# A two-layer GELU network on one core: the second matmul of the first superblocks as one pipeline with a pinned vector order, and a new start

## The chip, the cores and the metric

The kernel runs on one core of a Trainium2 chip. The metric is the device time of one execution in microseconds (us). The kernel before takes 1579.98 us (median of 3 runs, 1578.31 to 1580.16). The profile is of one execution; its span is about 2 us shorter than that execution's time. Engines: PE is the matmul engine, DVE the vector engine, ACT the scalar engine, POOL the general-purpose engine, SP the engine whose queue issues most loads.

## The reference

```python
# x: 8 x 1024 x 1024, w1: 1024 x 4096, w2: 4096 x 1024, all float32
h = x @ w1
h = 0.5 * h * (1 + np.tanh(np.sqrt(2 / np.pi) * (h + 0.044715 * h ** 3)))
return (h @ w2).astype(np.float32)
```

## The kernel before

The 8192 rows of x are handled in eight superblocks of 1024. In each, the *first matmul* makes `g = gelu(x @ w1)` and the *second matmul* makes `g @ w2`. Both are done as a Strassen-like scheme: seven products of half-size blocks instead of eight, at the price of sums and differences of blocks, which DVE makes. For product `m` the left operand is one of these (a single block, or the difference of two), and the right operand a sum of weight blocks:

```python
A_TERMS = {1: ("11", "22"), 2: ("21", "22"), 3: ("11", None), 4: ("22", None),
           5: ("12", "11"), 6: ("21", "11"), 7: ("12", "22")}
B_TERMS = {1: ("11", SUB, "22"), 2: ("11", None, None), 3: ("12", ADD, "22"), 4: ("21", ADD, "11"),
           5: ("22", None, None), 6: ("11", ADD, "12"), 7: ("21", ADD, "22")}
```

Superblock 0 reads float32 weights, casts them and keeps the float16 blocks in DRAM (`raw_d`, `raw2_d`; the profile leaves numbers out and calls both `raw_d`). Superblock 1 makes the sums that later superblocks load (`w_d`, `in_d`). From superblock 2 on, two products of the second matmul are cut once more in the same way; their parts are the *inner* products. So superblocks 0 and 1 do work that the other six don't; their second matmul is this:

```python
def matmul2_made(sb, g, keep_w1, xb):
    ...
    bring(("11", "21"), pool_copy, False)
    add(4)                                     # four sums on DVE, one per quarter of the weights
    for q, ps in product2(g, 4, pieces(4), pb, True, True):
        u[q] = temp()
        nc.vector.tensor_copy(out=u[q], in_=ps)
    bring(("22",), late_copy, True)
    bring(("12",), late_copy, True)
    keep(("21", "22", "11", "12"))             # 16 stores to raw2_d, in order on SP's queue
    for q, ps in product2(g, 2, pieces(2), pb, False):
        at, c21[q] = copy_out("21", q, ps)
        if q == 1 and sb == 0:
            xb = x_cast(sb + 1, at)            # the next superblock's x to float16, through DRAM
    add(1)
    for q, ps in product2(g, 5, pieces(5), qb, True):
        tt(u[q], u[q], ps, SUB)
        tt(d[q], u[q], c21[q], SUB)
    add(7, over="21")
    blocks = x_transpose(xb, load_in_order)    # 16 transposing DMAs, behind the stores on SP's queue
    ... # products 1, 7, 3, 6 in the same way

def product2(g, m, pieces, banks, first, by_chunk=False):
    ...
    for q in range(NQ):                        # four row groups
        a = g[u][:, :, cols]
        if v is not None:
            a = gcp.tile([P, NI, P], GT, name="gc")
            tt(a, g[u][:, :, cols], g[v][:, :, cols], SUB)
        for c in range(NI):
            mm(q, a[:, c, :], c)               # 16 matmuls of 128x512
        yield q, banks[q]

xs = x_first()                                 # superblock 0's x: load, transpose on PE, copy out
for sb in range(NSB):
    g, quad = matmul1(xs, sb)
    if sb < 2:
        xb = x_cast(sb + 1, last) if sb else None
        last, blocks = matmul2_made(sb, g, None if sb else quad.keep_raw, xb)
    ...
    if sb + 1 < NSB:
        xs = XOps(blocks)
        xs.make(5, 1, 2, 7, 6)                 # five x differences on DVE, 128x2048 each
```

`bring` loads and casts the weight blocks, `keep` stores them, and the banks (`pb`, `qb`, `rb`) hold PE's results until DVE or ACT copies or adds them.

The order of the code is not the order on an engine. A scheduler orders the instructions of each engine by its own simulation of when their inputs are ready. `keep_in_program_order(i)` ties `i` behind the instruction that the code created last for the same engine; an instruction that isn't tied may be put anywhere that its data allow.

## Time and profile before

The first matmul has 448 matmuls of 512 columns, and so has the second matmul of superblocks 0 and 1. Undisturbed they take 96.7 us (superblocks 2 to 7 show it), 0.2158 us per matmul. The table gives the time from the first matmul of a stage to that of the next, from the timeline of PE.

| stage | before, us | over 96.7 |
|---|---|---|
| start and first matmul, superblock 0 | 121.9 | |
| second matmul, superblock 0 | 100.0 | 3.3 |
| first matmul, superblock 1 | 103.6 | 6.9 |
| second matmul, superblock 1 | 97.3 | 0.6 |
| superblocks 2 to 7, and the end | 1154.1 | |

From the head of the page, kernel before: PE's busy time, its share of the 1576.8 us span, instructions, and the same for the other engines.

```profile
PE 1546.9 (98%) x7808; PEld 767.0 (49%) x7808; DVE 1015.0 (64%) x1276; ACT 468.6 (30%) x784; POOL 195.6 (12%) x282
```

The timeline of PE, kernel before. Columns: start, duration, engine, line, operation, operands, count; in brackets the idle time before it and what ended it. Neighbours are merged.

```profile
17.97 1.89 PE L285 MATMUL ps<-u 128*128 128x512 f16 x4 [2.45 <-DVE u L112]
...
33.91 36.46 PE L285 MATMUL ps<-u 128*128 128x512 f16 x167 [0.18 <-DVE tmp L112]
...
121.91 13.98 PE L568 MATMUL ps<-u,g 128*128 128x512 f16 x64
...
173.54 20.89 PE L568 MATMUL ps<-u,gc 128*128 128x512 f16 x96 [3.12 <-DVE gc L112]
...
221.90 9.66 PE L285 MATMUL ps<-u 128*128 128x512 f16 x44
235.94 27.12 PE L285 MATMUL ps<-u 128*128 128x512 f16 x116 [4.38 <-DVE tmp L112]
...
325.48 13.98 PE L568 MATMUL ps<-u,g 128*128 128x512 f16 x64
...
422.74 96.86 PE L285 MATMUL ps<-u 128*128 128x512 f16 x448
```

Up to 422.74 PE waits mainly in three places: in the start up to 33.9 us, 3.12 us for an operand difference (`gc`) in the second matmul of superblock 0, and 4.38 us early in superblock 1. Short waits between 33.9 and 121.9 us and one of 0.41 us at 339.87 (not shown) come on top. From 422.74 the stages are undisturbed, but for about 2 us near the end.

The timeline of all engines around the 4.38 us wait, kernel before:

```profile
223.90 0.55 POOL L381 DMA_DIRECT2D out_dram<-u  x1 [1.20 <-DVE u L112]
...
233.47 1.23 DVE L112 TENSOR_TENSOR u<-u 128x2048 f16<-128x2048 f16 x1 [6.60 <-DMA out_dram<-u]
...
235.94 14.37 PE L285 MATMUL ps<-u 128*128 128x512 f16 x58 [4.38 <-DVE tmp L112]
```

The table of stretches for the same time and for the start. Columns: stretch, its length, busy us (and count) of PE, PEld, DVE, ACT, POOL; then granted PE clock, DMA share, GB/s.

```profile
16.00:20.00 4.00, 1.89 (x4) 0.43 (x4) 2.95 (x4) 1.37 (x3) 2.00 (x2) 0.74 1.20 291
20.00:24.00 4.00, 3.35 (x12) 1.22 (x12) 3.89 (x5) 1.87 (x4) 1.72 (x3) 0.83 1.02 312
...
235.00:240.00 5.00, 4.06 (x12) 1.50 (x11) 3.46 (x6) 2.38 (x5) 2.96 (x6) 0.66 1.00 257
```

A weight sum at 233.47 stood 6.60 us at the head of DVE's queue, until a store of the output had landed and freed its buffer. What PE needed next was behind it. After the wait the clock was 0.66.

### The profile page before, as it was taken

How to read it: one execution, taken by the hardware profiler on the slowest of the kernel's cores; microseconds unless marked ns; L12 is line 12 of the kernel's file. 1: busy time of each engine (PE TensorE's matmuls, PEld its weight loads, DVE VectorE, ACT ScalarE, POOL GpSimd, SP SyncE). 2: the span in 40 equal slices, each digit the busy share in tenths (PEclk: the TensorE clock that was granted, in tenths of full speed). 3: DMA queues.
4: the chain of work that ended last, by engine and by line, in shares of the span. 5: the costliest groups of instructions: out<-in, count | busy, mean ns of one | idle time of the engine just before them, and what ended most of it. 6: DMA issues, size and time to landing. Idle time of an engine off the chain costs nothing.

```text
span 1576.8 us, 20365 instructions
## 1 busy us (share of the span) xinstructions
PE 1546.9 (98%) x7808; PEld 767.0 (49%) x7808; DVE 1015.0 (64%) x1276; ACT 468.6 (30%) x784; POOL 195.6 (12%) x282
## 2 busy tenths in 40 slices
PE   7999989999999999999999999999999999999998
PEld 4444444444444455444554455544554445544455
DVE  6875967779655567555765647556575556655564
ACT  4645014420144112441024410344004430144210
POOL 2241021022300012000120001200111001200000
PEclk9999999999999999999999999999999999999999
DMA  9999885585963568634696446954569455653164
GB/s 312 338 319 343 247 287 185 196 256 203 336 230 98 200 254 280 228 116 178 247 329 188 165 153 240 361 151 170 185 242 345 134 187 202 243 224 132 54 230 170
DMA packets 165778, 353.16 MB, mean 224 GB/s; under 512 B 72752, under 2 KB 78896, under 8 KB 164784
## 3 DMA queue, kind: packets, MB, share of 16 engines
q1 hardware_dynamic: 148240, 283.69, 51.9%
q0 software_dynamic: 17440, 68.17, 13.1%
q8 instruction: 61, 1.00, 0.2%
q14 instruction: 37, 0.30, 0.1%
HBM read 277.35 MB, written 89.13 MB: 232 GB/s over the span
## 4 chain that ended last, share of the span: by engine, by line
PE 79%; DMA 3%; DVE 3%; issue 1%; ACT 0%; SPq 0%; DVEq 0%
PE ps L285 41%; PE ps L568 31%; PE ps L524 6%; DMA u<-w_d 2%; DVE u L112 1%; DMA u<-raw_d 1%; DVE gc L112 1%; DVE tmp L112 1%; DMA u<-in_d 0%; DVE tmp L444 0%; ACT tmp L618 0%; SPq L381 0%; DVEq L112 0%; SPq L513 0%
## 5 line engine op out<-in xcount | busy, mean ns | idle before, releaser
L285 PE MATMUL ps<-u 128*128 128x512 f16 x3584 | 780.5, 380 | 10.9 <-DVE tmp L112 6.6
L112 DVE TENSOR_TENSOR tmp<-tmp,ps 128x512 f32<-128x512 f32 x564 | 385.6, 686 | 307.6 <-ACT tmp L349 117.2
L285 PEld LDWEIGHTS <-u 128*128 128x128 f16 x3584 | 351.0, 98 | 438.0 <-issue 14.3
L568 PE MATMUL ps<-u,gc 128*128 128x512 f16 x1792 | 389.6, 379 | 3.5 <-DVE gc L112 3.1
L568 PEld LDWEIGHTS <-gc 128*128 128x128 f16 x1792 | 175.3, 98 | 215.3 <-DVE gc L112 3.6
L295 ACT ACTIVATE g<-tmp 128x512 f16<-128x512 f32 x256 | 161.1, 630 | 293.8 <-DVE tmp L112 293.8
L568 PE MATMUL ps<-u,g 128*128 128x512 f16 x1024 | 223.6, 379 | 0.0
L295 ACT ACTIVATE g<-ps 128x512 f16<-128x512 f32 x256 | 151.8, 596 | 95.9 <-PE ps L285 95.7
L112 DVE TENSOR_TENSOR u<-u 128x2048 f16<-128x2048 f16 (+2 forms) x155 | 166.5, 1110 | 11.9 <-DMA out_dram<-u 6.6
L112 DVE TENSOR_TENSOR u<-u,ps 128x512 f32<-128x512 f32 x160 | 106.5, 681 | 85.4 <-ACT tmp L625 37.3
L568 PEld LDWEIGHTS <-g 128*128 128x128 f16 x1024 | 100.1, 98 | 119.6
L112 DVE TENSOR_TENSOR gc<-g,g 128x2048 f16<-128x2048 f16 x112 | 132.9, 1219 | 15.8 <-PE ps L568 15.8
L381 POOL DMA_DIRECT2D out_dram<-tmp x64 | 35.1, 549 | 811.9 <-ACT tmp L618 636.2
L524 PE MATMUL ps<-u,gc 128*128 128x256 f16 x960 | 110.4, 274 | 0.8
L349 ACT COPY tmp<-ps 128x512 f32<-128x512 f32 x128 | 72.9, 570 | 94.1 <-PE ps L285 94.1
L524 PEld LDWEIGHTS <-gc 128*128 128x128 f16 x960 | 94.3, 98 | 13.2 <-issue 1.9
L112 DVE TENSOR_TENSOR gc<-u 128x2048 f16<-128x2048 f16 x60 | 73.2, 1219 | 39.3 <-PE ps L568 39.3
L112 DVE TENSOR_TENSOR tmp<-ps,tmp 128x512 f32<-128x512 f32 x128 | 88.3, 690 | 6.1 <-PE ps L285 1.1
L112 DVE TENSOR_TENSOR u<-tmp,ps 128x512 f32<-128x512 f32 x24 | 16.5, 687 | 74.8 <-PE ps L568 65.1
L112 DVE TENSOR_TENSOR u<-g,g 128x2048 f16<-128x2048 f16 x48 | 59.5, 1278 | 0.0
L618 ACT COPY tmp<-ps 128x512 f32<-128x512 f32 x24 | 14.1, 586 | 152.0 <-PE ps L568 152.0
L625 ACT COPY tmp<-ps 128x512 f32<-128x512 f32 x24 | 14.0, 585 | 134.2 <-PE ps L568 132.8
(32 smaller groups left out, 349.0 us busy)
## 6 DMA issues: line engine op xcount, KB each, us to landing
u<-w_d SPq DMA_DIRECT2D x187, 512.0 KB, 7.9
u<-raw_d SPq DMA_DIRECT2D x130, 512.0 KB, 7.4
u<-in_d SPq DMA_DIRECT2D x84, 512.0 KB, 7.7
gc<-in_w_dram SPq DMA_DIRECT2D x48, 512.0 KB, 5.9
raw_d<-u SPq DMA_DIRECT2D x32, 512.0 KB, 10.3
out_dram<-tmp POOLq DMA_DIRECT2D x64, 256.0 KB, 3.3
w_d<-u POOLq DMA_DIRECT2D x32, 512.0 KB, 4.4
xb<-in_x_dram POOLq DMA_DIRECT2D x56, 256.0 KB, 11.4
```

The costliest lines, as they stand in the source:

```text
L112: nc.vector.tensor_tensor(out=out, in0=in0, in1=in1, op=op)
L285: nc.tensor.matmul(bank, lhsT=ops[m][:, k, cs], rhs=xs[m][:, k, :], start=(first and k == 0), stop=(k == KH - 1), skip_group_check=not first,)
L295: gelu_last[0] = nc.scalar.activation(out=g[b][:, c, :], in_=src, func=GELU)
L349: nc.scalar.copy(out=v, in_=pb)
L381: return queue.dma_start(out=out2[r0:r0 + P, o0:o0 + OH], in_=src)
L524: nc.tensor.matmul(bank[:, i * HO:(i + 1) * HO], lhsT=t[:, c, i * P:(i + 1) * P], rhs=y[j][:, c, :], start=(first and i == 0 and c == 0), ...
L568: nc.tensor.matmul(banks[q], lhsT=a, rhs=pieces[c // QC][:, c % QC, :], start=(first and c == 0), stop=(c == NI - 1), skip_group_check=not ...
L618: nc.scalar.copy(out=c21, in_=ps)
L625: nc.scalar.copy(out=c12, in_=ps)
```

## The change

Its intent: (1) in the second matmul of superblocks 0 and 1, make sums and operands two steps ahead of the matmuls, one sum per step and not four in a row, with the order of DVE *pinned* (tied by `keep_in_program_order`); a step is one row group of one product, 16 matmuls; (2) pin the weight sums of superblock 1 in the first matmul, and issue superblock 1's x cast later; (3) at the start put all x copies on ACT, half of four x differences ahead of the last x tiles, the first upper weight copies on ACT, and dummy matmuls between the x tiles, to keep the PE clock up.

```diff
-    def tt(out, in0, in1, op):
-        nc.vector.tensor_tensor(out=out, in0=in0, in1=in1, op=op)
+    def tt(out, in0, in1, op, pin=False):
+        i = nc.vector.tensor_tensor(out=out, in0=in0, in1=in1, op=op)
+        if pin:
+            tc.keep_in_program_order(i)
 ...   # MadeQuad.sum: pinned in superblocks 1 and 2
-            make_sum(self.ops, m, self.raw, KH, QW, sl)
+            make_sum(self.ops, m, self.raw, KH, QW, sl, not self.first)
 ...   # start
-                cast = (nc.scalar.copy, pool_copy)[b]
+                cast = pool_copy if b and c else nc.scalar.copy
 ...
+    def keep_clock(bank, n):
+        for _ in range(n):
+            tc.keep_in_program_order(
+                nc.tensor.matmul(bank, lhsT=idle[:, :P], rhs=idle, start=True, stop=True)
+            )
 ...
-                    eng = nc.vector.tensor_copy if k == 0 else nc.scalar.copy
-                    eng(
+                    nc.scalar.copy(
 ...
+                keep_clock(idle_bank, 2 if a else (1, 1, 1, 12)[q])
+                if a == 0 and q == 1:
+                    xs.make(5, 1, 7, 6, cols=slice(0, HT // 2))
 ...   # second matmul of superblocks 0 and 1
-        def add(m, over=None):
-            u, op, v = B_TERMS[m]
-            sums[m] = []
-            for q in range(NI // QC):
-                t = unit(QC, OH) if over is None else raw[over][q]
-                tt(t, raw[u][q], raw[v][q], op)
+        def add(m, q):
+            u, op, v = B_TERMS[m]
+            t = sums[m][q]
+            tt(t, raw[u][q], raw[v][q], op, True)
 ...
+        start(4)
+        for q in range(NI // QC):
+            add(4, q)
 ...
+        def prepare(i):
+            if i >= len(steps):
+                return
+            m, q, banks, first, sum_m, over, _ = steps[i]
+            if sum_m is not None:
+                if q == 0:
+                    start(sum_m, over)
+                add(sum_m, q)
+            ops[i] = operand2(g, m, q, True)
+
+        for i in range(2):
+            prepare(i)
+        for i, (m, q, banks, first, _, _, post) in enumerate(steps):   # products 2, 5, 1, 7, 3, 6
+            prepare(i + 2)
+            if first:
+                banks.append(psum())
+            matmuls2(banks[q], ops[i], pieces(m), first)
+            post(q)
 ...
-            xb = x_cast(sb + 1, last) if sb else None
+            xb = x_cast(sb + 1, quads[2].stored) if sb else None
```

More of the change, by code (lines that the diff above doesn't have):

```diff
@@ L125, with make_sum @@
     pool_last = [None]
-    def make_sum(ops, m, raw, rows, cols, sl=slice(None)):
+    def make_sum(ops, m, raw, rows, cols, sl=slice(None), pin=False):
         u, op, v = B_TERMS[m]
@@ L136, in make_sum @@
             ops[m] = unit(rows, cols)
-        tt(ops[m][:, :, sl], raw[u][:, :, sl], raw[v][:, :, sl], op)
+        tt(ops[m][:, :, sl], raw[u][:, :, sl], raw[v][:, :, sl], op, pin)
     gelu_last = [None]
@@ L155, in __init__ @@
         def __init__(self, q, first, store):
-            self.q, self.store, self.ops = q, store, {}
+            self.q, self.first, self.store, self.ops = q, first, store, {}
             self.raw = raw_units(KH, QW)
@@ L191, in sum @@
         def sum(self, m, sl=slice(None)):
-            make_sum(self.ops, m, self.raw, KH, QW, sl)
+            make_sum(self.ops, m, self.raw, KH, QW, sl, not self.first)
             if self.store:
-                nc.gpsimd.dma_start(out=w1_d[self.q][:, m - 1, :], in_=flat(self.ops[m]))
+                self.stored = nc.gpsimd.dma_start(out=w1_d[self.q][:, m - 1, :], in_=flat(self.ops[m]))
         def keep_raw(self):
@@ L217, in __init__, with make @@
             self[3], self[4] = blocks["11"], blocks["22"]
-        def make(self, *ms):
+        def make(self, *ms, cols=slice(None)):
             for m in ms:
                 u, v = A_TERMS[m]
-                self[m] = unit(KH, HT)
-                tt(self[m], self.blocks[u], self.blocks[v], SUB)
+                if m not in self:
+                    self[m] = unit(KH, HT)
+                tt(self[m][:, :, cols], self.blocks[u][:, :, cols], self.blocks[v][:, :, cols], SUB)
     def x_blocks():
         return {b: unit(KH, HT) for b in ("22", "21", "12", "11")}
+    def keep_clock(bank, n):
[3 more added lines that the diff above has]
+            )
     def x_first():
@@ L230, in x_first @@
         make_identity(nc, identity)
+        idle_bank = psum()
+        keep_clock(idle_bank, 7)
         blocks = x_blocks()
@@ L325, in matmul1 @@
             quads.append(MadeQuad(0, True, False))
-            xs.make(5)
+            rest = slice(HT // 2, HT)
+            xs.make(5, cols=rest)
             cs = quads[0].load_cols(0, 1)
@@ L330, in matmul1 @@
                 if m != 3:
-                    xs.make(m)
+                    xs.make(m, cols=rest)
                 quads[0].sum(m, cs)
@@ L372, in matmul1 @@
         finish(*late)
-        return g, quads[-1]
+        return g, quads
     def store(sb, b, q, src):
@@ L416, in keep, with start @@
                         load_in_order(raw2_d[q][:, BLOCKS.index(b), :], flat(raw[b][q]))
-        def add(m, over=None):
+        def start(m, over=None):
+            sums[m] = raw[over] if over else [unit(QC, OH) for _ in range(NI // QC)]
+        def add(m, q):
             u, op, v = B_TERMS[m]
-            sums[m] = []
-            for q in range(NI // QC):
-                t = unit(QC, OH) if over is None else raw[over][q]
-                tt(t, raw[u][q], raw[v][q], op)
-                sums[m].append(t)
-                if sb and m not in INNER:
-                    nc.gpsimd.dma_start(out=w2_d[q][:, m - 1, :], in_=flat(t))
+            t = sums[m][q]
+            tt(t, raw[u][q], raw[v][q], op, True)
+            if sb and m not in INNER:
+                nc.gpsimd.dma_start(out=w2_d[q][:, m - 1, :], in_=flat(t))
         def pieces(m):
@@ L435, in copy_out @@
             return store(sb, b, q, c), c
-        u, c21 = {}, {}
+        u, c21, at = {}, {}, {}
         d = halves()[1]
@@ L440, in matmul2_made @@
         bring(("11", "21"), pool_copy, False)
-        add(4)
+        start(4)
+        for q in range(NI // QC):
+            add(4, q)
         for q, ps in product2(g, 4, pieces(4), pb, True, True):
@@ L447, in matmul2_made @@
         keep(("21", "22", "11", "12"))
-        for q, ps in product2(g, 2, pieces(2), pb, False):
-            at, c21[q] = copy_out("21", q, ps)
-            if q == 1 and sb == 0:
-                xb = x_cast(sb + 1, at)
-        add(1)
-        for q, ps in product2(g, 5, pieces(5), qb, True):
-            tt(u[q], u[q], ps, SUB)
-            tt(d[q], u[q], c21[q], SUB)
-        add(7, over="21")
-        blocks = x_transpose(xb, load_in_order)
-        for q, ps in product2(g, 1, pieces(1), rb, True):
-            tt(d[q], d[q], ps, ADD)
@@ L460, in matmul2_made @@
-        if sb:
-            split_inner(7, pieces(7))
-        for q, ps in product2(g, 7, pieces(7), rb, False):
-            tt(u[q], u[q], ps, ADD)
-            store(sb, "11", q, u[q])
-        add(3, over="22")
-        add(6, over="11")
-        if sb:
-            split_inner(6, pieces(6))
-        for q, ps in product2(g, 3, pieces(3), qb, False):
-            copy_out("12", q, ps)
-        for q, ps in product2(g, 6, pieces(6), qb, False):
-            tt(d[q], d[q], ps, ADD)
-            last = store(sb, "22", q, d[q])
@@ L474, in matmul2_made, with out21, minus5, plus1 @@
-        return last, blocks
+        def out21(q):
+            at[q], c21[q] = copy_out("21", q, pb[q])
+        def minus5(q):
+            tt(u[q], u[q], qb[q], SUB, True)
+            tt(d[q], u[q], c21[q], SUB, True)
+        def plus1(q):
+            tt(d[q], d[q], rb[q], ADD, True)
+        def out11(q):
+            tt(u[q], u[q], rb[q], ADD, True)
+            store(sb, "11", q, u[q])
+        def out12(q):
+            copy_out("12", q, qb[q])
+        def out22(q):
+            tt(d[q], d[q], qb[q], ADD, True)
+            at["last"] = store(sb, "22", q, d[q])
@@ new lines, in matmul2_made @@
+        steps = []
+        for m, banks, first, sum_m, over, post in (
+            (2, pb, False, None, None, out21),
+            (5, qb, True, 1, None, minus5),
+            (1, rb, True, 7, "21", plus1),
+            (7, rb, False, 3, "22", out11),
+            (3, qb, False, 6, "11", out12),
+            (6, qb, False, None, None, out22),
+        ):
+            steps += [(m, q, banks, first, sum_m, over, post) for q in range(NQ)]
+        ops = {}
+        def prepare(i):
[7 more added lines that the diff above has]
+            ops[i] = operand2(g, m, q, True)
@@ new lines, in matmul2_made @@
+        for i in range(2):
[6 more added lines that the diff above has]
+            post(q)
+            if (m, q) == (2, 1) and sb == 0:
+                xb = x_cast(sb + 1, at[1])
+            if (m, q) == (5, NQ - 1):
+                blocks = x_transpose(xb, load_in_order)
+            if sb and q == NQ - 1 and m in (1, 3):
+                split_inner({1: 7, 3: 6}[m], pieces({1: 7, 3: 6}[m]))
@@ L476, in split_inner @@
+        return at["last"], blocks
     def split_inner(m, pieces):
@@ L561, in inner_product, with operand2, matmuls2 @@
         tt(part("22"), part("22"), pair(qb), ADD)
-    def product2(g, m, pieces, banks, first, by_chunk=False):
+    def operand2(g, m, q, pin=False):
         u, v = A_TERMS[m]
-        def mm(q, a, c):
+        cols = slice(q * P, (q + 1) * P)
+        if v is None:
+            return g[u][:, :, cols]
+        a = gcp.tile([P, NI, P], GT, name="gc")
+        tt(a, g[u][:, :, cols], g[v][:, :, cols], SUB, pin)
+        return a
+    def matmuls2(bank, a, pieces, first, cs=range(NI)):
+        for c in cs:
             nc.tensor.matmul(
-                banks[q],
-                lhsT=a,
+                bank,
+                lhsT=a[:, c, :],
                 rhs=pieces[c // QC][:, c % QC, :],
@@ L575, in mm, with product2 @@
             )
+    def product2(g, m, pieces, banks, first, by_chunk=False):
         if first:
@@ L581, in product2 @@
                 for q in range(NQ):
-                    for c in range(c0, c0 + QC):
-                        mm(q, g[u][:, c, q * P:(q + 1) * P], c)
+                    matmuls2(banks[q], operand2(g, m, q), pieces, first, range(c0, c0 + QC))
                     if c0 + QC == NI:
@@ L587, in product2 @@
         for q in range(NQ):
-            cols = slice(q * P, (q + 1) * P)
-            a = g[u][:, :, cols]
-            if v is not None:
-                a = gcp.tile([P, NI, P], GT, name="gc")
-                tt(a, g[u][:, :, cols], g[v][:, :, cols], SUB)
-            for c in range(NI):
-                mm(q, a[:, c, :], c)
+            matmuls2(banks[q], operand2(g, m, q), pieces, first)
             yield q, banks[q]
@@ L635, in matmul2 @@
         return last
+    idle = consts.tile([P, HT], DT, name="idle")
+    nc.vector.memset(idle, 0.0)
     warm = consts.tile([P, 1], F32, name="warm")
@@ L641 @@
     for sb in range(NSB):
-        g, quad = matmul1(xs, sb)
+        g, quads = matmul1(xs, sb)
         if sb < 2:
-            xb = x_cast(sb + 1, last) if sb else None
-            last, blocks = matmul2_made(sb, g, None if sb else quad.keep_raw, xb)
+            xb = x_cast(sb + 1, quads[2].stored) if sb else None
+            last, blocks = matmul2_made(sb, g, None if sb else quads[-1].keep_raw, xb)
         else:
```

## The prediction

> **What bounds it now.** The tensor engine. The page's busy table gives PE 98% of 1576.8 us. In the timeline of PE alone an undisturbed first matmul stage (448 matmuls of 512 columns) takes 96.7 us in superblocks 2 to 7, 0.2158 us per matmul. The change can win only time over that pace in the first 423 us:
>
> - start (18.0 to 33.9 us): 50 matmuls need 10.8 us and take 15.9, so 5.1 us lost. The waits name DVE (1.5, 0.7, 0.2 us). The table of stretches shows a granted clock of 0.74 at 16–20 us and 0.83 at 20–24, with DVE full from 20 to 32 us.
> - 33.9 to 121.9 us: about 2.1 us lost in short waits on DVE results.
> - second matmul of superblock 0 (121.9 to 221.9): 100.0 against 96.7, 3.3 lost. One wait, 3.12 us at 173.5, on an operand difference (gc): DVE was busy 40 of 40 us in 160–200, doing whole groups of weight sums ahead of it.
> - first matmul of superblock 1 (221.9 to 325.5): 103.6, so 6.9 lost: 4.38 us waiting at 235.9, then a clock of 0.66 in 235–240. DVE stood 6.6 us before a weight sum whose buffer waited for the last output store to land (223.9 to 233.4) while the DMA was full (share 1.0 to 1.16 in 225–235).
> - second matmul of superblock 1: 97.3, 0.6 lost.
>
> Sum about 18 us, 1.1%.
>
> **What the change does.**
> 1. Start. Eight x copies move from DVE (0.69 us) to ACT (0.58): ACT then needs 1.16 us per x tile, just under the 1.27 us at which tiles arrive, so x is not later. Halves of four differences (1.22 us whole) move before the last tiles: about 2.3 us less DVE after 16.3 us. The first upper weight copies go from POOL (1.04 us each) to ACT (0.57): 0.9 us sooner. Dummy matmuls keep the clock up: the Trainium skill's "TensorE: Matmul & The Clock Gate", Part 1, says the clock is throttled by default and activity releases it, and Part 4 that transposes don't count as activity; the trace agrees, the 0.74 follows the transposes. The 12 last dummies end (12 x 0.216 = 2.6 us after 15.5) about when the first weight sum is ready, 18 us. The first real matmul stays near 18 us (DMA full); gain 3.8 of 5.1 us. Later weight groups have 5 us or more of slack, so this should survive.
> 2. Second matmul, superblocks 0 and 1: sums are split one per step, operands made two steps ahead. DVE needs at most 1.2+1.2+1.3 us per 3.45 us step, with 3 us of lead. Gain 3.0 + 0.4.
> 3. Pinned weight sums no longer jump ahead, so no such sum stands before the output store; the x cast moves about 45 us later. The 4.38 us wait and its cold clock go; about 1 us of short waits stays. Gain 5.8 us.
>
> All is on the critical path. Sum 13.0 us: 1580 - 13 = 1567 us, range 1562 to 1574. Over 2% (below 1548) isn't there to win: chance 0.01; within 2% 0.98; slower 0.01.
>
> **Right if:** clock near 1.0 in 16–24 us; 112 matmuls done near 43 us (47.3 now); no gc wait near 170; second matmul of superblock 0 about 97 us; first of superblock 1 about 97.7 us; DVE's wait on the output store gone; from superblock 2 on the same, with the 2.0 us wait for an inner operand near the end.
>
> **Wrong if:** dummies delay transposes or the first product; ACT falls behind on x; pinning leaves DVE before a late load and stalls PE; the DMA-bound weight stream eats the earlier start.

## More of the kernel before

`issue_after(i)` ties a group behind `i`.

## The result, and the profile after

The changed kernel takes 1584.92 us (median of 4 runs, 1584.29 to 1585.43); the kernel before, in the same rounds, 1580.07. The ratio is 1.0032, with a 95% interval of 1.0015 to 1.0049. Here and below a ratio is the mean time of one kernel's fast runs over that of the kernel before in the same rounds, so not quite the ratio of the medians quoted. The change was forecast to win 13 us and cost 5.

| stage | before, us | after, us |
|---|---|---|
| start and first matmul, superblock 0 | 121.9 | 122.5 |
| second matmul, superblock 0 | 100.0 | 110.4 |
| first matmul, superblock 1 | 103.6 | 98.8 |
| second matmul, superblock 1 | 97.3 | 99.2 |
| superblocks 2 to 7, and the end | 1154.1 | 1152.7 |

The same line of the page, kernel after (span 1583.6 us; 30 of the matmuls are dummies), and then the timeline of PE, kernel after:

```profile
PE 1550.8 (98%) x7838; PEld 768.8 (49%) x7838; DVE 1011.6 (64%) x1273; ACT 474.6 (30%) x794; POOL 193.8 (12%) x280
```

```profile
19.36 4.27 PE L299 MATMUL ps<-u 128*128 128x512 f16 x19 [1.47 <-DVE u L112]
...
122.51 13.97 PE L624 MATMUL ps<-u,g 128*128 128x512 f16 x64 [1.91 <-DVE u L112]
138.40 51.97 PE L624 MATMUL ps<-u,gc 128*128 128x512 f16 x240 [1.92 <-DVE gc L112]
199.02 6.38 PE L624 MATMUL ps<-u,gc 128*128 128x512 f16 x16 [8.64 <-DVE gc L112]
205.24 13.98 PE L624 MATMUL ps<-u,g 128*128 128x512 f16 x64
...
232.87 96.86 PE L299 MATMUL ps<-u 128*128 128x512 f16 x448
331.64 13.97 PE L624 MATMUL ps<-u,g 128*128 128x512 f16 x64 [1.91 <-DVE u L112]
347.53 48.52 PE L624 MATMUL ps<-u,gc 128*128 128x512 f16 x224 [1.92 <-DVE gc L112]
```

Superblock 1's first matmul (232.87) now runs its 448 matmuls in one piece, 96.86 us: the 4.38 us wait is gone, as forecast. But there are five new waits. Four are of 1.9 us, at the start of product 4 (122.51, 331.64) and of product 2 (138.40, 347.53) in both superblocks. One is of 8.64 us, at 199.02; after it 16 matmuls take 6.22 us (199.02 to 205.24) where 16 x 0.2158 = 3.45 are due, 2.8 us more. The table of stretches of the kernel after has the clock there:

```profile
199.00:201.00 2.00, 1.98 (x5) 0.74 (x6) 2.00 (x3) 0.00 (x0) 0.01 (x1) 0.50 0.04 8
201.00:203.00 2.00, 2.00 (x6) 0.76 (x5) 2.00 (x3) 0.00 (x0) 0.53 (x1) 0.50 0.43 82
```

What DVE did at these waits, from the timeline of all engines, kernel after:

```profile
120.64 0.69 DVE L112 TENSOR_TENSOR tmp<-ps,tmp 128x512 f32<-128x512 f32 x1 [0.17 <-PE ps L299]
121.25 4.62 DVE L112 TENSOR_TENSOR u<-u 128x2048 f16<-128x2048 f16 x4
...
136.52 0.69 DVE L461 COPY tmp<-ps 128x512 f32<-128x512 f32 x1 [0.17 <-PE ps L624]
137.13 4.62 DVE L112 TENSOR_TENSOR gc<-g,g 128x2048 f16<-128x2048 f16 x4
...
181.79 1.22 DVE L112 TENSOR_TENSOR gc<-g,g 128x2048 f16<-128x2048 f16 x1
194.87 1.22 DVE L112 TENSOR_TENSOR u<-u 128x2048 f16<-128x2048 f16 x1 [11.86 <-DMA u<-xb]
...
197.75 1.22 DVE L112 TENSOR_TENSOR gc<-g,g 128x2048 f16<-128x2048 f16 x1
...
199.02 6.38 PE L624 MATMUL ps<-u,gc 128*128 128x512 f16 x16 [8.64 <-DVE gc L112]
```

At the borders, the sums of product 4 (121.25) start only after DVE's last result of the first matmul (120.64), though they can be made earlier (run 2 below does it); and the operands of product 2 (137.13) start only after the last copy of product 4's result (136.52). Each pinned instruction is tied to the one created last before it, and that one needs the last matmul of the stage that ends. PE, which had nothing left to do, waits out that last result and then one sum or one operand.

At the long wait, DVE stands still from about 183 to 194.87, and what it then starts is no sum of the pipeline: its right brackets name `u<-xb`, the x transposes. It is the first of the next superblock's x differences, unpinned, which the scheduler had put ahead of a pinned sum and its operand. The chain of waits of the kernel after shows the way from the stores to it (start, duration in us, what):

```profile
145.62 23.53 DMA raw_d<-u
...
192.10 2.65 DMA u<-xb
...
194.87 0.10 DVE u L112
...
199.02 34.01 PE ps L624 x144
```

So: 16 stores of weights on SP's queue, then the 16 transposes behind them, which SP issues one after the other from 169.24 to 193.4 us (24.1 us, not shown), then the x difference, and behind that on DVE the operand that PE needs. "TensorE: Matmul & The Clock Gate" in the Trainium skill, Part 1, says that DVE and ACT are strictly first in, first out; the operand's inputs had long been there, and it waited 11.86 us behind an instruction that it had nothing to do with.

### The profile page after: what moved, and what is told of

It reads as the page before. It is cut to its first block, busy times and chain, and to the rows that moved or that the text cites. A ratio compares the mean times of both kernels' runs of the same rounds, so it can differ in the third digit from the quotient of the medians.

```text
span 1583.6 us, 20425 instructions
## 1 busy us (share of the span) xinstructions
PE 1550.8 (98%) x7838; PEld 768.8 (49%) x7838; DVE 1011.6 (64%) x1273; ACT 474.6 (30%) x794; POOL 193.8 (12%) x280
## 4 chain that ended last, share of the span: by engine, by line
PE 87%; DMA 6%; DVE 3%; SPq 2%; issue 1%; ACT 0%; POOL 0%; DVEq 0%; ACTq 0%
PE ps L299 47%; PE ps L624 35%; PE ps L573 6%; SPq L122 2%; DVE u L112 2%; DMA raw_d<-u 2%; DMA u<-w_d 2%; DMA gc<-in_w_dram 1%; DVE gc L112 1%; DVE tmp L112 1%; DMA u<-in_d 0%; DMA u<-in_x_dram 0%; ACT u L149 0%; ACT g L309 0%; DMA u<-xb 0%
## 5 line engine op out<-in xcount | busy, mean ns | idle before, releaser
L364 ACT COPY tmp<-ps 128x512 f32<-128x512 f32 x128 | 72.9, 570 | 85.5 <-PE ps L299 85.4
L668 ACT COPY tmp<-ps 128x512 f32<-128x512 f32 x24 | 14.1, 587 | 151.9 <-PE ps L624 151.9
L449 ACT COPY tmp<-ps 128x512 f32<-128x512 f32 x16 | 9.4, 586 | 158.8 <-PE ps L624 158.8
## 6 DMA issues: line engine op xcount, KB each, us to landing
xb<-in_x_dram POOLq DMA_DIRECT2D x56, 256.0 KB, 11.6
```

The source lines that it names most:

```text
L364: nc.scalar.copy(out=v, in_=pb)
L449: nc.scalar.copy(out=c, in_=ps)
L668: nc.scalar.copy(out=c21, in_=ps)
```

## The experiments

Each time given is the median; the ratio is against the kernel before in the same rounds. Every result was correct.

### Run 1: the x differences later

Base: the kernel after. The x differences are issued behind the operand of step (6,1):

```diff
             ops[i] = operand2(g, m, q, True)
+            if (m, q) == (6, 1):
+                at["mark"] = tt_last[0]
 ...
-            xs.make(5, 1, 2, 7, 6)
+            with tc.issue_after(mark[0].ins):      # superblocks 0 and 1
+                xs.make(5, 1, 2, 7, 6)
```

> The changed kernel, with one thing different: the five x differences of the next superblock are put on the vector engine behind the operand of step (6,1). My theory: in the changed kernel one unpinned x difference sits in the vector queue ahead of a pinned sum and operand, waits 11.9 us for the x transposes, and so costs the tensor engine 8.6 us of waiting and about 2.8 us of cold clock after it. Then this run takes 1584.9 - 11.4 = 1573.5 us (1572 to 1575.5), faster than before, and no wait on a gc operand near 190 us is left. Rival: the pipeline itself asks too much of the vector engine (3.6 us of work in a step of 3.45 us), and the x difference only happens to stand where the lag shows: then less than 4 us is won (over 1581 us) and waits on gc operands remain in superblock 0.

Measured: 1573.30 us (1573.23 to 1574.01), ratio 0.9955 (0.994 to 0.997). The timeline of PE of this run:

```profile
121.57 13.97 PE L629 MATMUL ps<-u,g 128*128 128x512 f16 x64 [1.92 <-DVE u L112]
137.46 55.43 PE L629 MATMUL ps<-u,gc 128*128 128x512 f16 x256 [1.92 <-DVE gc L112]
...
220.35 96.86 PE L301 MATMUL ps<-u 128*128 128x512 f16 x448
```

The 256 matmuls of products 2, 5, 1 and 7 run in one piece of 55.43 us. The long wait is gone, with its slow clock, and the time fell by 11.6 us, where they had come to 11.4. DVE was busy 39.7 of 45 us in 160 to 205 and the pipeline kept up, so the rival falls: DVE wasn't overloaded; in the kernel after it stood still. The four border waits of 1.9 us stay.

### Run 2: the borders not pinned

Base: the kernel after.

```diff
-            tt(t, raw[u][q], raw[v][q], op, True)
+            tt(t, raw[u][q], raw[v][q], op, m != 4)
 ...
-            ops[i] = operand2(g, m, q, True)
+            ops[i] = operand2(g, m, q, i > 1)
```

> The changed kernel, with the four sums of product 4 and the first two operands of product 2 not pinned. My theory: the pins put them behind the last result of the stage before, so each of the four borders costs 1.9 us; without the pins the waits of 1.9 us at the start of product 4 and of product 2 go, in both superblocks. But in superblock 0 the later stall ends when the x transposes land, at a time that the DMA queue sets, so what is won before it is waited there: that wait grows from 8.6 to about 12.4 us, and only superblock 1 keeps its 3.8 us: 1581 us (1580 to 1582.5). Rival: the stall near 190 us is of vector work and keeps its length; then all four borders count, 1584.9 - 7.7 = 1577 us.

Measured: 1577.70 us (1576.70 to 1580.69), ratio 0.9980 (0.9963 to 0.9997). All four waits of 1.9 us are gone. The long wait, from the timelines of this run (all engines):

```profile
192.91 1.23 DVE L112 TENSOR_TENSOR u<-u 128x2048 f16<-128x2048 f16 x1 [13.12 <-DMA u<-xb]
...
197.06 6.22 PE L624 MATMUL ps<-u,gc 128*128 128x512 f16 x16 [9.91 <-DVE gc L112]
```

Neither expectation held. The wait grew, as my theory wanted, but from 8.64 to 9.91 us and not to 12.4. The time of landing was not fixed: the x difference ran at 192.91, two us earlier than in the kernel after (194.87), and the transposes on SP's queue began at 166.93 and not at 169.24. A likely reason, not tested: SP's queue itself waits for PE (12.1 us between 118 and 205 us in the kernel after), so it moves forward with PE. The rival's time was met, but its reason is refuted by run 1 and by the line above, where DVE waits 13.12 us for `u<-xb`. The profile is of the slowest of the four executions, 1580.69 us; the other three took 1576.70 to 1577.77. What the borders cost is read better from run 3 against run 1, which has no long wait: 1573.30 - 1565.39 = 7.9 us, where 7.7 were expected.

### Run 3: both edits

> Both edits together. My theory: 1584.9 - 11.4 - 7.7 = 1566 us (1564 to 1568.5), about 14 us faster than before, superblock 0's second matmul in about 97 us and superblock 1's in about 97 us. Rival (an overloaded vector engine): the waits move elsewhere in the second matmul and over 1572 us is left.

Measured: 1565.39 us (1565.25 to 1566.55), ratio 0.9906 (0.9891 to 0.9921). The timeline of PE:

```profile
119.56 13.98 PE L629 MATMUL ps<-u,g 128*128 128x512 f16 x64
133.37 55.42 PE L629 MATMUL ps<-u,gc 128*128 128x512 f16 x256
...
216.25 96.86 PE L301 MATMUL ps<-u 128*128 128x512 f16 x448
312.94 13.98 PE L629 MATMUL ps<-u,g 128*128 128x512 f16 x64
...
410.10 35.13 PE L301 MATMUL ps<-u 128*128 128x512 f16 x162
```

The expectation held, for the time and for both stages. Second matmul of superblock 0: 119.56 to 216.25, 96.7 us; first matmul of superblock 1: 96.7; second: 97.2. These stages are at the pace of undisturbed ones. This version beats both kernels by 0.9% or more.

### Run 4: both edits, with the old start

Run 3 with the start of the kernel before (x copies on DVE and ACT, no dummies, no half differences, upper weight copies on POOL).

> As the run with both edits, but with the start of the kernel before: x copies shared by vector and scalar engine, no dummy matmuls, no half differences ahead of time, weight copies on the pool engine. If the traces are read right, the new start won only 1.3 us by the end of the first stage: about 1567.5 us, 1 to 2 us over the run with both edits. If the new start is worth the 3.8 us of the prediction: about 1570 us. If it costs time: below the run with both edits.

Measured: 1568.21 us (1566.95 to 1569.15), ratio 0.9922 (0.9907 to 0.9936). That is 2.8 us over run 3, between the two guesses, and the intervals of the ratios overlap. A second measure is the moment when superblock 0's second matmul can start, less the border wait where there is one. With the old start, in four traces (before, runs 4, 5, 6), it is 121.9, 122.5, 123.4 and 122.2 us, mean 122.5; with the new start, in six (after, runs 1, 2, 3, 11, 12), 120.6, 119.7, 121.4, 119.6, 120.5 and 121.1, mean 120.5. The new start wins about 2 us, and one start differs from the next by nearly as much.

### Runs 5 and 6: what won superblock 1's first matmul?

Base of both: the kernel before. Run 5 issues only the x cast later (`x_cast(sb + 1, quads[2].stored)`); the queues of DVE, ACT, PE and SP are the same as before. Run 6 pins only the weight sums of superblock 1 (`make_sum(..., not self.first)`).

> The kernel before, with the x cast of superblock 1 issued behind the stored sums of quad 2 and nothing else (the vector, scalar and tensor queues are the same). Question: what won the 6.9 us of superblock 1's first matmul? If it was the cast's traffic that held up the last output store, the vector engine's wait on that store (6.6 us) shrinks below 2 us, the tensor engine's 4.4 us wait and its cold clock go, and the run takes about 1574.5 us. If it was the order of the sums (my theory), the store is only a little quicker, because three of the cast's eight pieces stood before nothing but time: 1577 to 1580 us.

> The kernel before, with the weight sums of superblock 1 (and of the first quad of superblock 2) pinned and the x cast left where it was. If the order of the sums is what counts (my theory): superblock 1's first matmul in about 97 us and 1580 - 6 = 1574 us (1573 to 1575.5). If the later cast is needed too: 1577 us or more.

Measured: run 5 1579.40 us (1577.87 to 1580.96), ratio 1.0000 (0.9983 to 1.0017); run 6 1576.23 us (1575.99 to 1577.58), ratio 0.9985 (0.9970 to 1.0000). DVE in run 5 (all engines), then PE in run 6:

```profile
236.42 1.22 DVE L112 TENSOR_TENSOR u<-u 128x2048 f16<-128x2048 f16 x1 [6.35 <-DMA out_dram<-u]
```

```profile
223.91 96.86 PE L287 MATMUL ps<-u 128*128 128x512 f16 x448
320.60 13.98 PE L570 MATMUL ps<-u,g 128*128 128x512 f16 x64
337.08 57.10 PE L570 MATMUL ps<-u,gc 128*128 128x512 f16 x256 [2.50 <-DVE tmp L446]
```

With the cast out of the way DVE still waits 6.35 us for the output store (6.60 before): the cast's traffic is not the cause. With the sums pinned and the cast left, superblock 1's first matmul takes 96.7 us. So the order of the sums is the cause, and the later cast is worth nothing measurable. Run 6 missed its number because the new order gave 4 us back: at 337.08 PE waits 2.50 us for the copies of product 4's banks, before which the scheduler had put four operands and five x differences (10.2 us of DVE work), and the second matmul of superblock 1 took 101.0 us. It is once more an unpinned block of work in the wrong place in DVE's queue.

### Runs 7 and 8: the start

Base: run 3. Run 7 ties the first weight copies on ACT behind the last x copies (`keep_in_program_order` on the copies of the first column). Run 8 cuts each dummy matmul to 8 columns (`rhs=idle[:, :8]`); the order of DVE and ACT work changed a little in the first stage.

> The run with both edits, with the first weight copies pinned on the scalar engine behind the last x copies. In the trace the first weight copy stands ahead of the last two x copies and makes them wait 1.2 us for its load, so the first product starts at 19.4 to 19.8 us and not at 18. If that order costs what it seems: the first product near 18.3 us, and 1 to 1.5 us less, about 1564.2 us. If the weight stream (full DMA) sets the pace: the wait moves to the next loads and the time stays at 1565.4 us.

> The run with both edits, with each dummy matmul cut to 8 columns, so that they keep nothing busy (the order of vector and scalar work changes a little in the first stage). If the clock is what they are for: granted clock of 0.5 to 0.8 in 19 to 24 us, and 1 to 3 us more than the run with both edits: 1566.5 to 1568.5 us. If the first products wait for loads and sums anyway, the slow clock hides behind these waits: within 0.7 us of it.

Measured: run 7 1567.77 us (1565.71 to 1568.35), ratio 0.9927 (0.9912 to 0.9942); run 8 1564.97 us (1564.29 to 1565.57), ratio 0.9912 (0.9897 to 0.9926). In run 7 the first product starts at 18.57 and not at 19.68, but then PE waits 2.23 us at 24.42 for a DVE result: nothing won. The trace shows why: on DVE a weight sum stands ahead of that result and waits 1.97 us for POOL's copy of a weight load, and POOL could start this copy only at 22.34 us (21.88 in run 3, 22.17 in run 12), when the load had landed. So the wait moved to the next loads, as the second guess had it. In run 8 the table of stretches shows the slow clock that the dummies were to prevent:

```profile
19.00:20.00 1.00, 1.00 (x5) 0.45 (x4) 1.00 (x4) 0.66 (x2) 0.00 (x0) 0.79 1.14 298
20.00:21.00 1.00, 1.00 (x3) 0.30 (x2) 0.88 (x3) 0.96 (x2) 0.00 (x0) 0.50 1.12 340
...
23.00:24.00 1.00, 1.00 (x6) 0.45 (x5) 0.56 (x2) 0.27 (x1) 0.40 (x1) 1.00 1.11 354
```

and no time was lost that shows: the second guess held, and the second matmul of superblock 0 could start at 119.2 us (119.6 in run 3). PE's waits for `tmp` results of DVE in the first 40 us fell from 2.4 us in run 3 to 1.5: slow matmuls filled time that is otherwise waited. One reserve: with the changed order of DVE and ACT the first product of run 8 began at 18.57, 1.1 us earlier than in run 3, which could hide a small loss; but run 7 began as early with a full clock and was no faster. The dummies keep the clock up (1.00 in 16 to 24 us of the kernel after), and no gain from it shows here.

### Runs 9 and 10: which part of the new start?

Base: run 3. Run 9 puts the first upper weight copies back on POOL, run 10 makes the four x differences whole, after the last x tiles.

> The run with both edits, with the first upper weight copies back on the pool engine (1.04 us each) instead of the scalar engine (0.57). The run with the old start was 2.8 us slower than the run with both edits; which part of the new start is that? Estimate from the copy times: the upper blocks are ready 0.9 us later, so 0.5 to 1 us more than the same kernel without this edit. If the vector work is what counts: no difference (within 0.5 us).

> The run with both edits, with the four x differences made whole after the last x tiles, as the kernel before makes them. It puts back 2.3 us of vector work after 16.3 us, where the vector engine is the one waited for: 1.5 to 2.5 us more than the run with both edits if the vector engine is the limit of the start; under 0.7 us if the weight loads are.

Measured: run 9 1567.02 us (1564.59 to 1567.37), ratio 0.9920 (0.9905 to 0.9935); run 10 1567.24 us (1566.20 to 1568.87), ratio 0.9929 (0.9916 to 0.9941). Run 3's kernel beside them on the same chip (run 12) took 1566.19 us, ratio 0.9921 (0.9907 to 0.9935). Differences of 0.8 and 1.0 us are within the spread of one kernel. Which part of the new start makes its 2 us is left open.

### Runs 11 and 12: the wait at the end, and run 3 again

All kernels wait about 2 us at the last superblock's first inner product. The chain of waits of the kernel before shows why:

```profile
1510.18 0.59 ACT tmp L618
...
1510.79 0.33 SPq L381
...
1511.21 4.35 DMA u<-in_d
```

L618 copies out product 2, L381 is its store on SP's queue (only the last superblock uses that queue for stores), and the load of an inner operand was behind it. Run 11 is run 3 with these four stores on POOL's queue: `queue = nc.gpsimd if sb < NSB - 1 or b == "21" else nc.sync`.

> The run with both edits, with the four output stores of block 21 in the last superblock put on the pool engine's queue, as in all other superblocks. In every trace the last superblock waits about 2 us (and again 0.4 to 0.6) at its first inner product, and the chain of waits goes: copy out of product 2, its store on the sync queue, the loads of inner operands queued behind it. If that order is the cause, these waits go, with the cold clock after them: 2 to 4 us less than the run with both edits. If the operands wait for buffers instead: no change.

> The run with both edits once more, unchanged, beside the three others on the same chip: 1565.4 us (1564 to 1567), 0.9% faster than before.

Measured: run 11 1562.68 us (1562.23 to 1563.35), ratio 0.9899 (0.9886 to 0.9913); run 12 1566.19 us (1564.82 to 1567.55). PE in run 11 has no wait after 410 us, and the 3.5 us between the two runs lie in the 2 to 4 that were expected. Run 11 is the fastest version found, 1.0% under the kernel before.

## Why the prediction was wrong

Forecast: 1567 us, from 13.0 us won. Measured: 1584.92 us.

- **Superblock 1's first matmul (5.8 us): right.** The 4.38 us wait and its slow clock went; without its border wait the stage is at 96.9 us, 6.7 less. Runs 5 and 6 show that the pinned sums did it. The later cast, which the forecast named beside them, won nothing measurable (run 5: ratio 1.0000).
- **The second matmul (3.0 + 0.4 us): here the forecast failed.** The step was "DVE needs at most 1.2+1.2+1.3 us per 3.45 us step, with 3 us of lead." The sum was right (3.7 us at most; the fullest steps of the kernel after, from 158.4 to 169.2 us, take 3.6): run 1 keeps PE's pace with no wait. What was missing is the order of the queue. The step took it that DVE would do this work in the order of the code, and did not ask what unpinned work the scheduler would put between. One x difference, which waits for the x transposes at the end of SP's queue, stood ahead of a sum and an operand: 11.86 us of standing still, 8.6 us of PE waiting and 2.8 us of slow clock. Run 1 takes exactly that away (11.6 us).
- **The same step left out what a pin costs at a border.** A pinned instruction is tied to the one created just before, even if that one ends the stage before. Four borders of 1.9 us, 7.7 us in all, were not in the sum. Run 2 removes them. The forecast's "pinning leaves DVE before a late load" named the danger in general, but gave it no term.
- **The start (3.8 us): mis-sized.** It won about 2 us (run 4 and the stage ends); in the profile of the kernel after, the first 112 matmuls were done at about 47 us, as before, and not at 43. The first product began there at 19.36 us and not near 18: on ACT the first weight copy, which waited 1.20 us for its load, stood ahead of the last two x copies. Run 7 mended that order and won nothing, because the next weight loads set the pace: the forecast's "DMA-bound weight stream eats the earlier start". The part of it that rested on the clock was wrong: the clock was 1.00 as forecast, yet run 8 without it was no slower.
- With both faults mended the forecast's time comes out: 1565.4 us in run 3 and 1566.2 in run 12. That it fits so closely is partly luck: in the profiles, run 3 against the kernel before won 2.35 us in the start (3.8 forecast), 3.3 and 0.1 in the second matmuls (3.0 and 0.4), 6.9 in superblock 1's first matmul (5.8) and 0.6 in the rest (none), and the misses cancel. In the kernel after, the two order faults took the gain back: 11.4 + 7.7 = 19.1 us, and 1584.9 - 19.1 = 1565.8.

What stays open: which part of the new start makes its 2 us (runs 9, 10).

## What to carry to other kernels

Where an engine works strictly in order, ask of each instruction in its queue what it can wait for, not only how long it takes: one early instruction that depends on a slow DMA stops all that stands behind it. Pinning part of a queue leaves the unpinned rest free to land in between, and ties the first pinned instruction of a stage to the end of the stage before; pin the steady part, leave the operands of the first steps free, and tie late-input work behind a named step. A slow clock costs only where PE isn't waiting anyway: 2.8 us after the long wait in the kernel after, nothing that shows in run 8's start.

## What the Trainium skill lacked or had wrong

- "TensorE: Matmul & The Clock Gate", Part 4, says that the full clock doesn't engage for transposes. In the kernel before nothing but transposes (of float32) runs on PE from 4.4 to 15.5 us: the weight loads of the first 16 take 3.28 us (205 ns each), and those of every later 8 take 0.86 us (107 ns each). Their pace doubled after 3.3 us, and the first record of a full clock in the packed trace (the views don't print it) stands at that moment, 7.70 us; so transposes alone did release it. My prediction took the trace to agree with the page, which was a misreading: the slow clock at 18 us followed a gap of 2.45 us. What Part 1 of the page says of the two clocks, half and full, did hold: 0.50 in 199 to 203 us of the kernel after, after 8.64 us of waiting.
- The table's granted clock reads 1.00 from 4 to 8 us in the kernel before, while the pace of the transposes was half until 7.7 us: before the trace's first record of the clock that column says nothing. No page read has it.
- No page read here tells what an in-order queue costs when a DMA-dependent instruction is put early; here it was 8.6 us of PE waiting and 2.8 us of slow clock.
